# Broadcast rows read from a DRAM copy, and stationary weights stored by the host in the order of the loads

## The chip, the cores and the metric

The kernel runs on one core of a Trainium2 chip. Five engines work side by side: TensorE (PE, with its weight loads PEld), VectorE (DVE), ScalarE (ACT), GpSimd (POOL) and SyncE (SP), which in this kernel issues every DMA. The metric is the device time of one launch in microseconds, the median of several runs.

## The reference

The reference is a first attention block and two hybrid layers over 512 tokens of width 1024, in float32. What matters here is where one row of numbers is needed on all 128 partitions.

```python
# first block: FoX attention, 8 heads of 64; 16 meta tokens in front, so 528 positions
log_f = jax.nn.log_sigmoid((f_logit + b_f).astype(jnp.float32))
cum = jnp.cumsum(log_f, axis=1).transpose(0, 2, 1)
...
decay = cum[:, :, q0:q0 + Q_BLOCK, None] - cum[:, :, None, :kend]
return jnp.where(kpos[None, :] <= qpos[:, None], s + decay, NEG_INF)

# hybrid layers, branch A: mLSTM, 4 heads of 128, forward and backward
dmat = jnp.where(lower, bt[..., :, None] - bt[..., None, :] + it[..., None, :], -jnp.inf)
...
sqk = jnp.einsum('bhtd,bhsd->bhts', qt, kt) * jnp.exp(dmat - mt[..., None])
```

In FoX a term of the key alone, `-cum`, is added to the scores of each head: one row of 528 numbers, the same for all queries. In branch A the term of the key is `i[s] - B[s]`, one row of 512 numbers for each head and direction. After FoX comes MLA in the first block; after A come the branches B, C and D in each hybrid layer, an output projection and a feed-forward network (FFN) of width 2816.

## The kernel before

**Splits.** Every weight is read in float32 into a tile `raw` (three buffers of 128 x 1024, 512 KB), and `split_w` (L216 to L223) makes two parts of it: ACT writes `whi` (L220), POOL writes `wlo = raw - whi` (L222). `mm3` (L247 to L249) then does three matmuls with the parts.

**Weights as the stationary operand.** `proj_t` works on blocks of 128 output features. `w_cols` (L235) is the generator of these blocks: for a contraction over 1024 it loads a 1024 x 128 piece of the matrix with `load_w` (L232), so that each partition receives 8 runs of 128 numbers (512 bytes). For the `w_up` matrices, with a contraction over 512, a load has 4 runs of 256 numbers. `d_cols`, for branch D, gathers the two components of a head with two DMAs of 256 KB each in runs of 64 numbers. Natural projections (`proj_n`), the output projections (`proj_resid`) and `w_ffn_down` load in other ways.

**Rows.** `row_bcast` (L365) reads one SBUF row, which lies on one partition, 128 times, and writes it to all partitions:

```python
nc.sync.dma_start(dst, bass.AP(tensor=row.tensor, offset=row.offset, ap=[list(row.ap[0]), [0, P], [1, n]]))
```

FoX calls it once for each of the 8 heads, from `row` (8 partitions) to `cb`, which DVE adds to the scores (L918). Branch A calls it twice for each of 4 heads, from `arow` to `cst`; POOL adds the masks to it (L1332, tile `t`), and ACT takes exponentials of `t` and `cst` (L1349, L1352), which DVE multiplies with the scores (L1354).

**Order.** The order of TensorE is that of the program: `overlap` puts steps of the projections of later units between the steps of an attention. The other engines, and SP's DMAs, have an order that the scheduler fixes when the program is built; each runs its own list in order, so that an instruction that waits holds up what stands behind it. All DMAs are in SP's one list.

Of the kernel before, what the change touches and what calls it, by code (L numbers as in the profile page):

```python
# [18 lines left out]
P = 128  # L19
S = 512  # L20
D = 1024
KD = D // P
NT = S // P
# [7 lines left out]
# attention steps: how far the scores run ahead, and the values and the rest behind  # L31
# [6 lines left out]
# PE time given to the next work in each step after the last scores, and between the queries of branch B  # L38
# [4 lines left out]
# column offsets in the two input projections  # L43
# [4 lines left out]
# neighbourhood attention, tokens column by column: keys (in whole blocks of 128) of each tile of 128 queries  # L48
C_LO = (0, 0, 128, 256)
C_HI = (256, 384, 512, 512)  # L50
# the masks of the two inner tiles are the same
# [21 lines left out]
class Stream:  # L73
    """Projections in program order, doled out in small steps between the steps of an attention."""
# [4 lines left out]
    def push(self, gen, cost, paced=True, soon=False):  # L79
        """soon: right after the task at hand."""  # L80
        t = Task(gen, cost)
        t.paced = paced
        if soon and self.queue:
            self.queue.insert(1, t)
        else:
            self.queue.append(t)
        return t
# [26 lines left out]
    def pace(self, room, deadlines):  # L114
        """Work per unit of room, of which `room` is left, for tasks that must be done within less of it."""
# [12 lines left out]
def overlap(k, maps, look, lag, after=None, lead=4, tail=TAIL):  # L128
    """Work for after them begins with the last scores. Steps of an attention: scores run `look` maps ahead of the transposes, values and the rest `lag` behind.
    A map is (scores, transposes, values, rest, needs), needs a list of (stage, function that returns a task)."""  # L130
# [20 lines left out]
def late_steps(fns):  # L151
    """The last of the steps completes the last tile of tokens, and is not ready at once."""
    return [*fns[:-1], (0, S // 2), fns[-1], (S // 2, S)]
# [11 lines left out]
def hybrid_kernel(ctx: ExitStack, tc: tile.TileContext, i: dict, out: bass.AP):  # L165
# [40 lines left out]

    def evict_split(ps, hi, lo, scale=None):
        """hi + lo = scale * ps"""
# [7 lines left out]
    def split_w(src):  # L216
        """src [P, a, b], a * b <= 512"""
# [17 lines left out]
    def w_cols(ap, nk, c0, ncol):  # L235
        """Yields blocks of 128 output features, [P, nk, 128]."""
        width = 1024 // nk // P * P
        for a in range(0, ncol, width):
            raw = load_w(ap, 0, nk, c0 + a, min(width, ncol - a))
            for m in range(0, min(width, ncol - a), P):  # L240
                yield raw[:, :, m:m + P]

# [1 line left out]

    def mm3(ps, sh, sl, mh, ml, first, last):
        """ps += s @ m, from the parts of both"""
        T_.matmul(ps, sh, mh, start=first, stop=False)  # L247
        T_.matmul(ps, sh, ml, start=False, stop=False)  # L248
        T_.matmul(ps, sl, mh, start=False, stop=last)  # L249

    def proj_t(outs, raw, nk):
        """outs: (ps[feature, token], operand getter) for one block of features."""
# [12 lines left out]
    def proj_late(outs, ws, nk, step):  # L265
        """The same while the last tokens are still on their way: k.late lists ranges of tokens and the steps that complete them.
        The low parts of the tokens land last."""
# [12 lines left out]
    def proj_n(outs, ap, nk, c0, ncol, k0=0, more=None):  # L280
        """outs: (ps[token, ncol], operand getter); contraction over nk blocks of 128 rows of ap.
        more [P, nk, m]: the last m columns."""
# [21 lines left out]

    def rstd(ss, n, width, rows=P):
        """(ss / n + eps) ** -0.5"""
# [14 lines left out]
    # zeros, ones and powers of two are the same in both formats  # L321
# [5 lines left out]
    def softmax(src, dst):  # L327
        """dst = exp(src - max) over the row; returns its sum and the sum's reciprocal."""
# [6 lines left out]
    def softmax_banks(parts, dst):  # L335
        """The same from one or two banks (ps, first column, last); returns the sum's reciprocal."""
# [12 lines left out]
    def silu2(src, g):  # L349
        """g = 2 * silu(src) = src * (tanh(src / 2) + 1)."""  # L350
# [5 lines left out]
    def log_sigmoid(x, tmp):  # L356
        """x = min(x, 0) - log(1 + exp(-|x|))"""
# [5 lines left out]
    def row_bcast(dst, row, n):  # L363
        """One SBUF row to all partitions."""
        nc.sync.dma_start(dst, bass.AP(tensor=row.tensor, offset=row.offset, ap=[list(row.ap[0]), [0, P], [1, n]]))  # L365

# [11 lines left out]
    def to_stacks(th, tl, q, dst, n=S, off=0):  # L378
        """Split features of two heads [2*64, n]: q -> [hi; lo], k -> [hi; hi] and [lo; lo]."""
# [13 lines left out]
    class Head:  # L393
        """Attention output of one 64-wide head, [value, query], from the transposed weights of pairs of query tiles.

        v(block) -> [keys, 128] holding [v_hi | v_lo]; blocks(t) -> key blocks of query tile t."""
# [4 lines left out]
        def trans(self, t, p, col):  # L401
            """p [query, key] -> split [key, query]; col(block): first column of p."""
# [20 lines left out]
        def pv(self, t):  # L423
            """After the second tile of a pair; after the second pair the output goes to SBUF."""
# [20 lines left out]
    def pair_out(heads):  # L445
        """Outputs of two heads, [v_hi part; v_lo part] each, to one block [2*64, S]."""
# [12 lines left out]
    def y_block(yn, dst, gate=None, scale=None):  # L459
        """Natural y [P, NT, 128] to one transposed, split and gated block."""  # L460
# [10 lines left out]
    def trans_n(p):  # L471
        """p [query, S keys] -> split [key, query]"""
# [7 lines left out]
    def pv_n(pts, v):  # L480
        """ps[query, 256] = P @ [v_hi | v_lo], with the low part of P onto the first half."""
# [8 lines left out]

    def add_resid(x, t, half, ps, ss=None):
        """x += ps, and its sum of squares once x is final."""
# [10 lines left out]
    def act():  # L503
        """All positions, the meta tokens first."""
# [8 lines left out]
    def gain_row(ap, tag):  # L513
        """A gain along the features on all partitions, in halves."""
# [5 lines left out]
    def norm_tile(x, t, ss, dst, gain):  # L520
        """RMS norm of x [P, D], tile t of the tokens, into split and transposed form; returns the transposes as a second step."""
# [13 lines left out]
    def proj_resid(get, ap, k0, nk, on_tile, delay=1):  # L535
        """Natural projection to all D features that ends tile by tile; on_tile(t, halves) may return a second step, for `delay` tiles later."""
# [95 lines left out]
def first_body(k, fb, col, hl):  # L632
# [18 lines left out]
    def nat_pairs(outs, ap, nk, c0, ncol, put):  # L651
        """Tasks of a natural projection of two token tiles at a time; put(t, ps) returns a second step that follows the next pair.
        Returns the last of these steps."""
# [28 lines left out]
    # FoX forget gates: rows of -cum  # L682
    fl, ft = new(fb, [P, L], "row")[0:8], k.p_tile(L)[0:8]

    def forget(src, meta):
        """src [P, NT, 8], meta [16, 8]: natural projections"""
# [8 lines left out]
        V.tensor_scalar(fl, ft, -1.0, None, ALU.mult)  # L695

# [13 lines left out]
    def scores(t, pairs, mask):  # L710
        """128 queries against the first n positions, the mask on the last 128 of them."""
# [23 lines left out]
    qw, kw, gw = (k.w_cols(w_in, KD, c, 512) for c in (FQ, FK, FG))  # L735
# [18 lines left out]
    def fox_values():  # L754
        """With the forget gates, whose columns follow the values'."""
# [33 lines left out]
    gws = k.w_cols(w_in, KD, MG, 512)  # L789
    gates = []  # L790

    def low_rank_tile(t, ps):
        """c_q | c_kv | k_r of one tile: normed, rotated, then transposed."""
# [7 lines left out]
        # k_r lands on columns 64-95 of a block of 96  # L801
# [102 lines left out]
    def fox_head(hd):  # L904
# [5 lines left out]
        def sc(t):  # L910
            if t == 0:
                st.cb = new(pool, [P, L], "cb")
                k.row_bcast(st.cb, fl[hd:hd + 1, :], L)
# [927 lines left out]
```

## Time and profile before

| | |
|---|---|
| median of 3 runs | 2705.22 us (2703.84 to 2706.31) |
| span of the profiled execution, first to last instruction | 2704.8 us |
| mean granted TensorE clock over the span | 0.980 |
| busy: PE, DVE, ACT, POOL | 2577.5, 1333.4, 1161.4, 1286.3 us |

The time of the profiled execution itself is not among the three; its span lies 0.4 us under their median, so span and median can be used for one another here. An engine's busy time is the union of its instructions; the rest of the span it waits or has nothing to do. [...] The first block runs to about 346 us, the first hybrid layer to about 1510 us, the second to the end.

### The profile page before, as it was taken

To read this page: it belongs to the slowest core of one execution; us is meant where nothing else is said; L and a number is where in the kernel's file an instruction comes from. 1 tells how busy PE (TensorE), PEld (TensorE's weight loads), DVE (VectorE), ACT (ScalarE), POOL (GpSimd) and SP (SyncE) were. 2 spreads that over 40 slices of the span, in tenths; PEclk is the share of its full clock that TensorE was granted. 3 is DMA by queue.
4 is the path that set the end of the run, shared out by engine and by line. 5 is a ranking of instruction groups with operands and counts; after the bars stand their busy time and mean duration, and the time that the engine had idled before them with its cause. 6 is when DMAs were issued, how large, how long until landed. Compare 5 with 4: busy or idle time off the path is not lost.

```text
span 2704.8 us, 36334 instructions
## 1 busy us (share of the span) xinstructions
PE 2577.5 (95%) x12918; PEld 2137.9 (79%) x12918; DVE 1333.4 (49%) x2895; ACT 1161.4 (43%) x2533; POOL 1286.3 (48%) x1112
## 2 busy tenths in 40 slices
PE   7989987999999999999999988999999999999998
PEld 7777876787887887788888777778878878788887
DVE  3467644867645548332222347767345574322223
ACT  4457643445644445332223334356445453322223
POOL 3344243543365553545555445432655534455554
PEclk9989988999999999999999989999999999999999
DMA  5883247622346533423333367223465443333332
GB/s 142 111 136 82 59 122 80 69 87 74 90 129 164 137 92 99 137 84 100 94 94 95 108 63 87 76 83 85 126 149 140 101 106 123 95 100 94 94 94 94
DMA packets 354421, 276.81 MB, mean 102 GB/s; under 512 B 48816, under 2 KB 308144, under 8 KB 354240
## 3 DMA queue, kind: packets, MB, share of 16 engines
q1 hardware_dynamic: 354240, 274.49, 43.2%
q8 instruction: 102, 1.67, 0.3%
q14 instruction: 79, 0.65, 0.1%
HBM read 223.90 MB, written 6.29 MB: 85 GB/s over the span
## 4 chain that ended last, share of the span: by engine, by line
PE 70%; DVE 9%; DMA 8%; POOL 5%; issue 4%; ACT 3%; SPq 1%; POOLq 0%; ACTq 0%; DVEq 0%
PE A L247 15%; PE A L248 15%; PE A L249 15%; PE A L296 4%; PE A L295 4%; PE A L297 4%; PE A L313 4%; DMA raw<-in_w_in_dram 3%; PE A L440 2%; POOL wlo L222 2%; DMA raw<-in_w_out_dram 1%; DMA cst<-arow 1%; DVE ptl L211 1%; PE A L277 1%; DVE sm L330 1%
## 5 line engine op out<-in xcount | busy, mean ns | idle before, releaser
L222 POOL TENSOR_TENSOR wlo<-raw,whi 128x512 fp32r<-128x512 f32 (+2 forms) x721 | 921.8, 1281 | 937.7 <-ACT whi L220 927.7
L220 ACT CAST whi<-raw 128x512 fp32r<-128x512 f32 (+2 forms) x733 | 444.0, 608 | 805.5 <-PE A L248 435.1
L249 PE MATMUL A<-hi,wlo 128*128 128x512 f32 (+1 forms) x1848 | 729.5, 395 | 36.1 <-POOL wlo L222 30.1
L247 PE MATMUL A<-hi,whi 128*128 128x512 f32 (+1 forms) x1848 | 747.3, 404 | 7.0 <-ACT whi L220 6.3
L248 PE MATMUL A<-lo,whi 128*128 128x512 f32 (+1 forms) x1848 | 729.4, 395 | 0.4 <-DVE lo L211 0.4
L249 PEld LDWEIGHTS A<-hi,wlo 128*128 128x128 f32 x1848 | 351.8, 190 | 121.1 <-POOL wlo L222 35.6
L247 PEld LDWEIGHTS A<-hi,whi 128*128 128x128 f32 x1848 | 351.8, 190 | 73.2 <-ACT whi L220 7.6
L248 PEld LDWEIGHTS A<-lo,whi 128*128 128x128 f32 x1848 | 352.0, 190 | 64.6 <-DVE lo L211 0.6
L313 PE MATMUL A<-ident,p 128*128 128x128 f32 (+3 forms) x1125 | 180.0, 282 | 30.9 <-DVE p L524 19.7
L494 DVE TENSOR_TENSOR x<-x,A 128x512 f32<-128x512 f32 x176 | 119.9, 687 | 154.5 <-PE A L297 96.8
L313 PEld LDWEIGHTS A<-ident,p 128*128 128x128 f32 (+3 forms) x1125 | 138.6, 142 | 71.4 <-DVE p L524 19.1
L211 DVE TENSOR_TENSOR ptl<-A,pth 128x512 fp32r<-128x512 f32 (+3 forms) x256 | 148.9, 583 | 81.4 <-ACT pth L210 80.4
L331 ACT ACTIVATE p<-p,sm 128x512 f32<-128x512 f32 (+6 forms) x160 | 100.7, 629 | 173.6 <-DVE sm L330 173.3
L353 DVE SCALAR_TENSOR_TENSOR t<-t,A 128x512 f32<-128x512 f32 x44 | 30.2, 687 | 251.8 <-ACT t L352 251.8
L210 ACT CAST pth<-A 128x512 fp32r<-128x512 f32 (+3 forms) x256 | 127.3, 501 | 55.4 <-PE A L313 54.8
L309 POOL TENSOR_TENSOR rstd<-rstd,mhalf 128x1 f32<-128x1 f32 (+2 forms) x80 | 56.0, 701 | 195.6 <-DVE rstd L308 191.5
L295 PE MATMUL A<-whi,hi 128*128 128x256 f32 (+7 forms) x440 | 146.2, 332 | 0.2
L296 PE MATMUL A<-wlo,hi 128*128 128x256 f32 (+7 forms) x440 | 143.4, 326 | 2.4 <-POOL wlo L222 2.4
L297 PE MATMUL A<-whi,lo 128*128 128x256 f32 (+7 forms) x440 | 143.0, 325 | 0.0
L1064 DVE SCALAR_TENSOR_TENSOR t<-A,t 128x512 f32<-128x512 f32 x44 | 30.4, 692 | 172.0 <-PE A L249 172.0
L295 PE MATMUL A<-whi,yh 128*128 128x512 f32 x288 | 112.1, 389 | 0.0
L296 PE MATMUL A<-wlo,yh 128*128 128x512 f32 x288 | 112.1, 389 | 0.0
(365 smaller groups left out, 4572.6 us busy)
## 6 DMA issues: line engine op xcount, KB each, us to landing
raw<-in_w_in_dram SPq DMA_DIRECT2D x154, 512.0 KB, 4.0
raw<-in_w_ffn_gate_dram SPq DMA_DIRECT2D x44, 512.0 KB, 3.9
raw<-in_w_ffn_up_dram SPq DMA_DIRECT2D x44, 512.0 KB, 3.8
raw<-in_w_ffn_down_dram SPq DMA_DIRECT2D x44, 512.0 KB, 3.7
raw<-in_w_out_dram SPq DMA_DIRECT2D x24, 512.0 KB, 3.5
raw<-in_w_in_dram SPq DMA_DIRECT2D x34, 256.0 KB, 3.6
ks<-sth SPq DMA_DIRECT2D x64, 128.0 KB, 2.4
ks<-stl SPq DMA_DIRECT2D x64, 128.0 KB, 2.3
```

The costliest lines, as they stand in the source:

```text
L210: A_.copy(hi, ps)
L211: V.tensor_tensor(lo, ps, f(hi), ALU.subtract)
L220: A_.copy(hi, src)
L222: (V if k.lo and k.turn % k.lo == 0 else G).tensor_tensor(lo, src, f(hi), ALU.subtract)
L247: T_.matmul(ps, sh, mh, start=first, stop=False)
L248: T_.matmul(ps, sh, ml, start=False, stop=False)
L249: T_.matmul(ps, sl, mh, start=False, stop=last)
L295: T_.matmul(ps, sh, wh[:, j], start=(b + j == 0), stop=False)
L296: T_.matmul(ps, sh, wl[:, j], start=False, stop=False)
L297: T_.matmul(ps, sl, wh[:, j], start=False, stop=(b + j == nk - 1))
L313: T_.transpose(dst, src, ident[0:k, 0:k])
L494: V.tensor_tensor(xx, xx, ps, ALU.add)
```

## The change

Rows: the eight rows of FoX (`row`, 8 x 528) and the rows of branch A (`arow`, 36 x 512) are written once to a tile in DRAM when they are complete, and every broadcast reads its row from that copy. Weights: the host stores each matrix that `w_cols` reads as an array `t_...` in which a load is one block, and each partition's part of it is one run of 1024 numbers (4096 bytes); `d_cols` goes, and its two DMAs for a head become one. The number of bytes that are loaded is the same. Comments and docstrings are removed too, which moves line numbers.

```diff
-    def w_cols(ap, nk, c0, ncol):
-        width = 1024 // nk // P * P
-        for a in range(0, ncol, width):
-            raw = load_w(ap, 0, nk, c0 + a, min(width, ncol - a))
-            for m in range(0, min(width, ncol - a), P):
-                yield raw[:, :, m:m + P]
+    def w_cols(ap):
+        loads, _, per, nk, _ = ap.shape
+        for a in range(loads):
+            raw = raw_tile().rearrange("p (m k c) -> p m k c", m=per, k=nk)
+            nc.sync.dma_start(raw, ap[a])
+            for m in range(per):
+                yield raw[:, m]
...
-    def row_bcast(dst, row, n):
-        nc.sync.dma_start(dst, bass.AP(tensor=row.tensor, offset=row.offset, ap=[list(row.ap[0]), [0, P], [1, n]]))
+    def rows_out(rows, tag):
+        r = new(dram, list(rows.shape), tag)
+        nc.sync.dma_start(r, rows)
+        return r
...
         V.tensor_scalar(fl, ft, -1.0, None, ALU.mult)
+        fox.rows = k.rows_out(fl, "frows")
...
-    qw, kw, gw = (k.w_cols(w_in, KD, c, 512) for c in (FQ, FK, FG))
+    qw, kw, gw = (k.w_cols(i["t_" + n]) for n in ("fq", "fk", "fg"))
...
-                k.row_bcast(st.cb, fl[hd:hd + 1, :], L)
+                nc.sync.dma_start(st.cb, fox.rows[hd].partition_broadcast(P))
...
-    gw = k.w_cols(i["w_ffn_gate_2"][l], KD, 0, DFF)
-    uw = k.w_cols(i["w_ffn_up_2"][l], KD, 0, DFF)
+    gw, uw = (k.w_cols(i[n][l]) for n in ("t_gate", "t_up"))
...
         br.rows = mx, bc
+        br.arows = k.rows_out(a, "arows")
...
-                k.row_bcast(hs.ab[:, d], a[32 * d + hd:32 * d + hd + 1, :], S)
+                nc.sync.dma_start(hs.ab[:, d], br.arows[32 * d + hd].partition_broadcast(P))
...
-    def d_cols(c0):
-        for hd in range(4):
-            raw = k.raw_tile().rearrange("p (k c d) -> p k c d", k=KD, c=2)
-            for c in range(2):
-                a = c0 + 256 * c + 64 * hd
-                nc.sync.dma_start(raw[:, :, c], w.w_in[:, a:a + 64].rearrange("(k p) c -> p k c", p=P))
-            yield raw.rearrange("p k c d -> p k (c d)")
-
-    qw, kw = d_cols(DQ), d_cols(DK)
+    qw, kw = (k.w_cols(i["t_" + n][l]) for n in ("dq", "dk"))
...
+def _blocks(w, c0=0, n=None, per=1):
+    n = w.shape[-1] - c0 if n is None else n
+    *lead, rows, _ = w.shape
+    w = w[..., c0:c0 + n].reshape(*lead, rows // P, P, n // (P * per), per, P)
+    o = len(lead)
+    return np.ascontiguousarray(w.transpose(*range(o), o + 2, o + 1, o + 3, o, o + 4))
...
+    for n in "abcd":
+        out["t_up_" + n] = _blocks(g[f"w_up_{n}_2"], per=2)
+    out["t_gate"], out["t_up"] = _blocks(g["w_ffn_gate_2"]), _blocks(g["w_ffn_up_2"])
```

Apart from names and line numbers, PE, DVE and ACT keep their order. SP's and POOL's lists change at the places below.

SP's list at the start of branch A's attention in the first hybrid layer, before: two rows of each of two heads (`cst` from `arow`) stand in front of the next weight loads.

```order
L232 DMA raw_4948<-in_w_in_dram 128x8x128
L232 DMA raw_5012<-in_w_in_dram 128x8x128
L232 DMA raw_5066<-in_w_in_dram 128x8x128
L365 DMA cst_4918<-arow_4402 128x1x512 x2
L365 DMA cst_5210<-arow_4402 128x1x512 x2
L232 DMA raw_5134<-in_w_in_dram 128x8x128
L232 DMA raw_5247<-in_w_in_dram 128x8x128
L232 DMA raw_5352<-in_w_in_dram 128x8x128
L365 DMA cst_5521<-arow_4402 128x1x512 x2
```

The same place now:

```order
L240 DMA raw_4952<-in_t_aq_dram 128x1024
L240 DMA raw_5016<-in_t_ak_dram 128x1024
L240 DMA raw_5070<-in_t_ao_dram 128x1024
L367 DMA arows_4756<-arow_4404 36x512
L1334 DMA cst_4922<-arows_4756 128x512 x2
L240 DMA raw_5138<-in_t_aq_dram 128x1024
L1334 DMA cst_5214<-arows_4756 128x512 x2
L240 DMA raw_5251<-in_t_ak_dram 128x1024
L240 DMA raw_5356<-in_t_ao_dram 128x1024
L1334 DMA cst_5525<-arows_4756 128x512 x2
```

The copy (L367) is new, and the first read of it waits until it has landed; a weight load now stands ahead of the second head's rows.

POOL's list at the same place, before: `t` is the row with the mask, `wlo` the low part of a weight.

```order
L222 TENSOR_TENSOR wlo_4951<-raw_4948,whi_4950 128x512
L1332 TENSOR_TENSOR t_1038_4919<-cst_4918,masks_160 128x512
L222 TENSOR_TENSOR wlo_4967<-raw_4948,whi_4966 128x512
L1332 TENSOR_TENSOR t_1039_4920<-cst_4918,masks_160 128x512
L222 TENSOR_TENSOR wlo_5015<-raw_5012,whi_5014 128x512
```

And now:

```order
L222 TENSOR_TENSOR wlo_4955<-raw_4952,whi_4954 128x512
L222 TENSOR_TENSOR wlo_4971<-raw_4952,whi_4970 128x512
L1336 TENSOR_TENSOR t_1040_4923<-cst_4922,masks_160 128x512
L1336 TENSOR_TENSOR t_1041_4924<-cst_4922,masks_160 128x512
L222 TENSOR_TENSOR wlo_5019<-raw_5016,whi_5018 128x512
```

One `wlo` has moved ahead of the first `t`, so that it no longer stands behind the wait for a row. The second hybrid layer differs in the same way.

## Rows read from the trace of the kernel before

**Rows 1.** The page: busy time of the engines; PE and its clock in 40 slices.

```profile
PE 2577.5 (95%) x12918; PEld 2137.9 (79%) x12918; DVE 1333.4 (49%) x2895; ACT 1161.4 (43%) x2533; POOL 1286.3 (48%) x1112
...
PE   7989987999999999999999988999999999999998
...
PEclk9989988999999999999999989999999999999999
```

**Rows 2.** DMA issues: count, KB of each, median us from issue to landing.

```profile
raw<-in_w_in_dram SPq DMA_DIRECT2D x154, 512.0 KB, 4.0
...
raw<-in_w_out_dram SPq DMA_DIRECT2D x24, 512.0 KB, 3.5
...
cst<-arow SPq DMA_DIRECT2D x16, 256.0 KB, 20.3
...
cb<-row SPq DMA_DIRECT2D x8, 264.0 KB, 11.8
cb<-in_norm_dram SPq DMA_DIRECT2D x8, 256.0 KB, 3.4
...
spill<-v SPq DMA_DIRECT2D x4, 512.0 KB, 2.9
```

**Rows 3.** Chain of work that ended last, 425 to 470 us: start, us, what.

```profile
425.68 11.85 DMA cst<-arow
...
443.43 24.16 DMA raw<-in_w_in_dram
```

**Rows 4.** Timeline of POOL, 425 to 455 us: start, us, instruction, [idle before, releaser].

```profile
437.66 1.26 POOL L1332 TENSOR_TENSOR t<-cst,masks 128x512 f32<-128x512 f32 x1 [12.56 <-DMA cst<-arow]
438.88 1.26 POOL L222 TENSOR_TENSOR wlo<-raw,whi 128x512 fp32r<-128x512 f32 x1
```

**Rows 5.** Timeline of PE, branch A of the first hybrid layer.

```profile
440.20 0.79 PE L249 MATMUL A<-hi,wlo 128*128 128x512 f32 x1 [6.54 <-POOL wlo L222]
...
451.46 0.80 PE L249 MATMUL A<-hi,wlo 128*128 128x512 f32 x1 [6.07 <-POOL wlo L222]
...
468.36 0.50 PE L247 MATMUL A<-hi,whi 128*128 128x512 f32 x1 [1.80 <-ACT whi L220]
```

**Rows 6.** Timeline of PE, branch A of the second hybrid layer.

```profile
1598.77 0.80 PE L249 MATMUL A<-hi,wlo 128*128 128x512 f32 x1 [6.39 <-POOL wlo L222]
...
1608.40 0.79 PE L249 MATMUL A<-hi,wlo 128*128 128x512 f32 x1 [3.56 <-POOL wlo L222]
...
1627.82 0.80 PE L247 MATMUL A<-hi,whi 128*128 128x512 f32 x1 [4.24 <-ACT whi L220]
```

**Rows 7.** Timeline of PE in FoX.

```profile
87.52 0.52 PE L717 MATMUL A<-ks,qs 128*128 128x272 f32 x2 [1.55 <-DVE stl L214]
...
139.52 0.69 PE L313 MATMUL A<-ident,p 128*128 128x128 f32 x2 [4.95 <-DVE p L918]
...
208.72 0.47 PE L440 MATMUL A<-yl,vm 16*64 16x256 f32 x1 [2.69 <-DVE yl L211]
```

**Rows 8.** Windows, nine stretches after those idle times; first, last, sum.

```profile
88.45:91.80 3.35, 3.35 (x8) 2.22 (x8) 2.09 (x8) 2.42 (x9) 1.28 (x1) 0.50 0.96 141
...
1627.82:1631.21 3.39, 3.26 (x7) 2.15 (x8) 2.79 (x7) 1.67 (x3) 2.52 (x2) 0.50 1.14 135
sum 39.23, PE 39.09 PEld 30.52 DVE 26.45 ACT 17.50 POOL 15.43; mean PE 4.34 PEld 3.39 DVE 2.94 ACT 1.94 POOL 1.71
```

A row of windows gives start and end, length, busy time (count) of PE, PEld, DVE, ACT and POOL, the granted clock, the DMA engines' share and GB/s.

**Rows 9.** Timeline of PE, two more idle times in FoX.

```profile
168.05 0.51 PE L717 MATMUL A<-ks,qs 128*128 128x264 f32 x2 [1.28 <-DVE p L918]
...
189.83 0.51 PE L717 MATMUL A<-ks,qs 128*128 128x264 f32 x2 [1.17 <-DVE yl L211]
```

**Rows 10.** Timeline of PE, at the start of a later head of branch A.

```profile
1692.31 0.52 PE L249 MATMUL A<-hi,wlo 128*128 128x512 f32 x1 [2.24 <-POOL wlo L222]
```

**Rows 11.** Windows, a stretch of the first FFN (columns as above).

```profile
1350.00:1395.00 45.00, 45.00 (x197) 36.65 (x196) 9.60 (x14) 13.29 (x22) 24.11 (x20) 1.00 0.34 100
```

**Rows 12.** Waits: engine and line, what it waited for, us in total, times, longest.

```profile
ACT whi L220 <- DMA raw<-in_w_in_dram: 37.0, 12, 9.4
```

More of the change, by code (lines that the diff above doesn't have):

```diff
@@ L788, in first_body @@
     ckh, ckl = new(fb, [P, L], "ckh", F32R), new(fb, [P, L], "ckl", F32R)
-    gws = k.w_cols(w_in, KD, MG, 512)
+    gws = k.w_cols(i["t_mg"])
     gates = []
@@ L1114, in mixers @@
     w_in = i["w_in_2"][l]
-    glw = k.w_cols(w_in, KD, GL, 4 * D)
+    glw = k.w_cols(i["t_gl"][l])
     T_COST = 3 * KD * k.pe_cost(S)
@@ L1133, in up @@
     def up(b, y, ready=()):
-        uw = k.w_cols(i["w_up_" + "abcd"[b] + "_2"][l], 4, 0, D)
+        uw = k.w_cols(i["t_up_" + "abcd"[b]][l])
         for m in range(KD):
@@ L1296, in gate_cols @@
         A_.activation(flo, pv[:, 1], AF.Exp, scale=-1.0)
-    qw, kw, ow = (k.w_cols(w.w_in, KD, c, 512) for c in (AQ, AK, AO))
+    qw, kw, ow = (k.w_cols(i["t_" + n][l]) for n in ("aq", "ak", "ao"))
     taps = col("conv").rearrange("p (j t) -> p j t", j=8)
@@ L1571, in branch_c @@
     br.y = []
-    qw, kw, vw = (k.w_cols(w.w_in, KD, c, 512) for c in (CQ2, CK2, CV2))
+    qw, kw, vw = (k.w_cols(i["t_" + n][l]) for n in ("cq", "ck", "cv"))
     def by_col(ap):
@@ L1795, in _layout @@
            "norm1": g["norm1_g_2"], "norm2": g["norm2_g_2"]}
-    for n in ("w_in_2", "w_up_a_2", "w_up_b_2", "w_up_c_2", "w_up_d_2", "w_out_2", "w_ffn_gate_2", "w_ffn_up_2", "w_ffn_down_2"):
+    for n in ("w_in_2", "w_out_2", "w_ffn_down_2"):
         out[n] = g[n]
+    for n, c0 in (("fq", FQ), ("fk", FK), ("fg", FG), ("mg", MG)):
+        out["t_" + n] = _blocks(g["w_in"][0], c0, 512)
+    w2 = g["w_in_2"]
+    for n, c0, m in (("aq", AQ, 512), ("ak", AK, 512), ("ao", AO, 512), ("cq", CQ2, 512), ("ck", CK2, 512), ("cv", CV2, 512), ("gl", GL, 4 * D)):
+        out["t_" + n] = _blocks(w2, c0, m)
+    for n, c0 in (("dq", DQ), ("dk", DK)):
+        w = w2[:, :, c0:c0 + 512].reshape(N_LAYERS, D, 2, 4, 64).transpose(0, 1, 3, 2, 4).reshape(N_LAYERS, D, 512)
+        out["t_" + n] = _blocks(w)
+    for n in "abcd":
+        out["t_up_" + n] = _blocks(g[f"w_up_{n}_2"], per=2)
+    out["t_gate"], out["t_up"] = _blocks(g["w_ffn_gate_2"]), _blocks(g["w_ffn_up_2"])
     first = np.zeros((P, NCOL_FIRST), f32)
```

## The prediction

> **What bounds the kernel now.** I read the page first. TensorE is busy 95% of the span: 2577.5 of 2704.8 us [rows 1]. So it is the bound nearly everywhere, and a change that touches no matmul can win at most the 127 us in which it stands still, and the time that it loses at the low clock level. The slices tell where these lie: PE is below 9 tenths, and its granted clock below full, at the start, in FoX (slices 2 and 3, about 135 to 270 us), in branch A of the first hybrid layer (slices 5 and 6) and in branch A of the second (slices 23 and 24). In between both rows are nines.
>
> The table of DMA issues says what is special in FoX and branch A. A row broadcast of 256 KB takes 20.3 us in the median from issue to landing, one of 264 KB in FoX 11.8 us, while weight loads of 512 KB land in 3.5 to 4.0 us [rows 2]. The chain of work that ended last shows both sides of it at the start of branch A: the first broadcast, issued at 425.68 us, is waited for 11.85 us, and a weight load issued at 443.43, behind four of them, takes 24.16 us instead of 4.0 [rows 3]. So the transfers of one SBUF row are slow, and the queue behind them is late too.
>
> The timeline of POOL links this to TensorE: POOL stands 12.56 us at the first `t` (L1332) until the row has landed, and the next `wlo` stands behind it [rows 4]. TensorE, whose matmul needs that `wlo`, is idle 6.54 us, then 6.07 us at the second broadcast, then 1.80 us for the late weight load [rows 5]. The second hybrid layer repeats it with 6.39, 3.56 and 4.24 us [rows 6]. In FoX three idle times follow a broadcast: 1.55 us (at the split of a projection whose weights were queued behind two rows), 4.95 us and 2.69 us (at what DVE makes of scores and `cb`) [rows 7].
>
> [...]
>
> **The change part by part.** *The rows' idle time.* It removes the slow reads. The nine idle times sum to 6.54 + 6.07 + 1.80 = 14.41, 6.39 + 3.56 + 4.24 = 14.19 and 1.55 + 4.95 + 2.69 = 9.19, in all 37.8 us [rows 5 to 7].
>
> *The clock after them.* Work at half the clock takes twice its time, so half of 39.09 us, 19.5 us, comes back if TensorE no longer stops there [rows 8]. Gross gain: 57.3 us.
>
> *What is added.* Three copies of rows to DRAM, and a wait for each in SP's list before the first read; behind that wait stand the other row reads and the next weight loads. The trace has no such small copy. From above, a store of 512 KB to DRAM lands in 2.9 us [rows 2]; from below it is nothing. I take the upper end, since the size is small against what makes up that time in no row I have. A broadcast out of DRAM is in the trace: a 256 KB gain row, read for all partitions by the same call, lands in 3.4 us [rows 2]. So the first row of a group is there 2.9 + 3.4 = 6.3 us after `arow` is ready instead of 11.85, and the others right behind it instead of some 10 us later each.
>
> Does that close the 6.54 us? TensorE ran dry at 440.20 - 6.54 = 433.7 us. In the new order one `wlo` more is done before POOL stands at `t`; it feeds 12 matmuls of 0.23 us (45.00 us for 197, [rows 11]), 2.7 us, to 436.4. The row lands at 425.7 + 6.3 = 432.0, two `t` and a `wlo` take 3 x 1.26 us [rows 4], which gives 435.8. So this wait goes, narrowly, and the second and third, for later rows and the queue, with room.
>
> *What stays.* At later heads of branch A, where the row had landed long before, TensorE still stops up to 2.24 us, since POOL does two `t` and another subtraction ahead of the `wlo` [rows 10]. The same can now show at the two first heads in each layer: 0 to 2.24 us, four times, 0 to 9 us. I take 1 us each, 4 us, since the arithmetic above comes out near zero for the first head. Such a stop can again cost a stretch at the half clock: I take 2 us in all, and up to 7 us. Sum of what stays: 6 us, at most 16.
>
> *Two more idle times in FoX*, 1.28 and 1.17 us, follow DVE and ACT work that was late behind broadcasts, but also behind other work [rows 9]. I take half, 1.2 us, with 0 to 2.45 as bounds.
>
> *The weight layout.* A load in 4 KB runs already exists: `w_out`, 512 KB in 3.5 us, against 4.0 us for `w_in` in runs of 512 bytes [rows 2]. So each changed load may land 0.5 us sooner. That is worth nothing where a load has cover: three buffers of `raw` let SP issue a load two loads ahead of its use, and in the FFN TensorE is busy 45.00 of 45.00 us [rows 11]. If the cover is gone, it is worth 0.5 us per wait: ACT waited 12 times for such a load, 37.0 us in all [rows 12], mostly behind rows and counted above. Bounds 0 to 6 us; I take 0, as ACT's other waits have slack before PE. [...]
>
> *Sum.* 57.3 - 6 + 1.2 + 0 = 52.5 us. The profiled span is 0.4 us under the median, so I take it off the median: 2705.2 - 52.5 = 2652.7, say **2653 us**. Best case: 57.3 + 2.45 + 6 = 65.8 us, 2639. Worst case of this mechanism: 57.3 - 16 and half of FoX's part lost (its 9.19 and half of its 12.8 us at the low clock make 15.6; half is 7.8), 33.5 us, 2672.
>
> **The rivals.** *A: another engine takes the place.* DVE, ACT and POOL are busy 43 to 49% of the span [rows 1], in FoX and branch A in chains of small instructions, and their lists are in order. If each row wait turned into waits on these chains, only the waits over 4 us would go (6.54, 6.07, 6.39, 4.24, 4.95: 28.2 us), half of that given back later, and half of the clock's part: 14 + 10 = 24 us, 2681. For it: the residual stops [rows 10]. Against it: these engines stood still themselves during the waits, POOL for 12.56 us at a time [rows 4], so they have the time.
>
> *B: the reads stay slow*, because 128 reads of one row meet in one place of DRAM as they met in one partition. Then only the layout is left: 0 to 6 us, 2702, within noise or just out of it. The gain row's 3.4 us speaks against it [rows 2]: same call, same size, also one row read 128 times. [...]
>
> *C: slower, by the weight loads.* The FFNs read 88 changed loads (22 blocks, gate and up, two layers) while TensorE has no slack at all [rows 11]. If a load in 4 KB runs landed so late that its cover was gone, each would stop TensorE. The gain of 52.5 us is used up when a load is 0.6 us late beyond its cover, at 88 x 0.6 = 53 us; at 1 us late the time is 2705 + 35 = 2740. Against it: `w_out` in such runs lands sooner, not later [rows 2].
>
> **How the numbers follow.** My forecast (33 to 66 us faster): 0.74. A (10 to 33 us): 0.14. More than 66 us, if other small stops in FoX go too: 0.06. B: 0.03. C: 0.03. The range reaches half of A: 2632 to 2678. 0.2% of the time is 5.4 us, about what a measurement can tell from no change. Faster takes the forecast, A and the larger gain, 0.94, and a little of B: 0.95; the same 0.02, slower 0.03.
>
> **What the profile after would show.** Row broadcasts landing in 3 to 5 us, copies in under 3 us; no wait of POOL for `cst` above 7 us; the six idle times of branch A gone or under 2.3 us; granted clock near 1.00 in the slices of branch A; changed weight loads at about 3.5 us, with the FFN windows unchanged at 197 matmuls in 45 us. Wrong if the broadcasts land in 10 us or more (B), if PE's idle time in branch A stands under other names, DVE or POOL (A), or if the FFN windows hold fewer matmuls (C).

## The result, and the profile after

| | before | after |
|---|---|---|
| median of 4 runs each, us | 2704.5 (2701.6 to 2706.3) | 2637.6 (2636.2 to 2640.0) |
| ratio, 95% interval | | 0.9753 (0.9740 to 0.9767) |
| span of the profiled execution, us | 2704.8 | 2635.8 |

The kernel is 66.9 us faster, where 52.5 us were forecast; 2637.6 lies in the range of 2632 to 2678, but past the best case of 65.8 us (2639). The first place to look is the page of the changed kernel, beside [rows 1].

```profile
PE 2554.8 (97%) x12918; PEld 2127.0 (81%) x12918; DVE 1334.6 (51%) x2895; ACT 1162.8 (44%) x2533; POOL 1291.5 (49%) x1112
...
PE   7999989999999999999999999999999999999998
...
PEclk9999999999999999999999999999999999999999
```

The dents of FoX and of both branches A are gone; slice 5 (counted from 0), before branch A begins, keeps its 8. The page also splits the 69.0 us of the two spans. The span less TensorE's busy time was 2704.8 - 2577.5 = 127.3 us and is 2635.8 - 2554.8 = 81.0: 46.3 us less standing still. The busy time itself fell by 22.7 us with the same 12918 matmuls. Most of that is the clock: windows over every stretch with a granted clock of 0.50 (a share of full speed), their sums before and after:

```profile
sum 107.66, PE 86.94 PEld 73.61 DVE 59.01 ACT 45.58 POOL 38.27; mean PE 3.95 PEld 3.35 DVE 2.68 ACT 2.07 POOL 1.74
...
sum 57.02, PE 52.76 PEld 44.69 DVE 32.88 ACT 19.47 POOL 19.18; mean PE 3.52 PEld 2.98 DVE 2.19 ACT 1.30 POOL 1.28
```

TensorE did 86.9 us of work at that level before and does 52.8 us now. Half of the difference, 17.1 us, is my estimate of what the clock gave back: at the first head of branch A in the changed kernel, matmuls of one size started 0.43 us apart at a granted clock of 0.50 (411.4 to 414.4 us) and 0.23 us apart at 1.00 (414.8 to 421.7 us), about twice as far. The cause of the other 5.6 us is not shown. Fewer stops may be part of it (72 of over 0.1 us instead of 100), since the matmul at 468.36 in [rows 5], behind a stop of 1.80 us, lasted 0.50 us, and the one at 419.46 below, with no stop before it, 0.39.

The DMA issues answer to [rows 2] (count, KB of each, median us from issue to landing):

```profile
raw<-in_t_gate_dram SPq DMA_DIRECT2D x44, 512.0 KB, 3.4
...
cst<-arows SPq DMA_DIRECT2D x16, 256.0 KB, 4.6
...
cb<-frows SPq DMA_DIRECT2D x8, 264.0 KB, 3.9
```

Rows land in 4.6 and 3.9 us instead of 20.3 and 11.8. POOL's timeline at the first head of branch A answers to [rows 4] (start, us, instruction, idle before and what ended it):

```profile
406.13 1.83 POOL L222 TENSOR_TENSOR wlo<-raw,whi 128x512 fp32r<-128x512 f32 x1 [1.06 <-ACT whi L220]
411.80 1.27 POOL L1336 TENSOR_TENSOR t<-cst,masks 128x512 f32<-128x512 f32 x1 [3.84 <-DMA cst<-arows]
413.36 1.28 POOL L1336 TENSOR_TENSOR t<-cst,masks 128x512 f32<-128x512 f32 x1 [0.29 <-DMA cst<-arows]
414.60 1.29 POOL L222 TENSOR_TENSOR wlo<-raw,whi 128x512 fp32r<-128x512 f32 x1
```

POOL waits 3.84 us where it waited 12.56. TensorE there and at the last head:

```profile
409.18 0.22 PE L314 MATMUL A<-ident,p 36*128 36x36 f32 x1 [1.00 <-DVE p L1288]
...
419.46 0.39 PE L250 MATMUL A<-hi,wlo 128*128 128x512 f32 x1
...
490.21 0.80 PE L250 MATMUL A<-hi,wlo 128*128 128x512 f32 x1 [2.25 <-POOL wlo L222]
```

The matmul at 419.46 is the one that stood still 6.07 us in [rows 5]; nothing precedes it now. Its `wlo` was ready at 414.60 + 1.29 = 415.89, so the slack is 3.6 us. The stop of 2.25 us at the last head (behind POOL's fourth pair of `t`, at 484.18 us) is of the kind in [rows 10], which is the same place in the second layer.

Since TensorE's order is the same in both kernels, a stretch can be cut at the same two instructions. Windows of FoX and the two branches A, first of the kernel before (start and end, length, busy time and count of PE, PEld, DVE, ACT and POOL, granted clock, DMA share, GB/s):

```profile
80.00:245.96 165.96, 148.67 (x839) 123.48 (x838) 105.52 (x301) 90.20 (x247) 71.37 (x76) 0.92 0.71 122
424.98:599.93 174.95, 149.46 (x766) 122.75 (x765) 116.17 (x309) 70.54 (x154) 80.42 (x73) 0.94 0.60 73
1580.02:1760.01 179.99, 156.31 (x797) 129.34 (x796) 119.58 (x311) 71.04 (x155) 84.45 (x75) 0.92 0.58 71
```

and of the changed kernel:

```profile
81.12:227.96 146.84, 139.54 (x840) 118.47 (x838) 106.15 (x299) 90.02 (x245) 69.64 (x76) 0.97 0.45 128
404.94:557.92 152.98, 145.93 (x766) 122.28 (x765) 116.70 (x309) 70.49 (x154) 81.95 (x73) 0.96 0.26 84
1535.70:1691.97 156.27, 148.20 (x798) 124.75 (x796) 120.26 (x311) 71.09 (x155) 85.79 (x75) 0.97 0.26 83
```

FoX is 19.1 us shorter, the two branches A 22.0 and 23.7; that leaves 69.0 - 64.8 = 4.2 us for the rest of the program. VectorE, ScalarE and POOL are as busy as before in the shorter stretches, and the DMA engines' share in branch A falls from 0.60 to 0.26. The FFN is what it was in [rows 11], again 197 matmuls in 45 us:

```profile
1309.00:1354.00 45.00, 45.00 (x197) 36.65 (x196) 9.59 (x14) 13.29 (x22) 24.15 (x20) 1.00 0.29 94
```

### The profile page after: what moved, and what is told of

It reads as the page before. It is cut to its first block, busy times and chain, and to the rows that moved or that the text cites. A ratio compares the mean times of both kernels' runs of the same rounds, so it can differ in the third digit from the quotient of the medians.

```text
span 2635.8 us, 36300 instructions
## 1 busy us (share of the span) xinstructions
PE 2554.8 (97%) x12918; PEld 2127.0 (81%) x12918; DVE 1334.6 (51%) x2895; ACT 1162.8 (44%) x2533; POOL 1291.5 (49%) x1112
## 4 chain that ended last, share of the span: by engine, by line
PE 75%; DVE 10%; POOL 4%; issue 4%; DMA 3%; ACT 2%; SPq 0%; POOLq 0%; DVEq 0%; ACTq 0%
PE A L248 17%; PE A L249 16%; PE A L250 16%; PE A L296 5%; PE A L297 5%; PE A L298 5%; PE A L314 4%; PE A L443 3%; POOL wlo L222 2%; DMA raw<-in_w_out_dram 1%; DVE ptl L211 1%; DMA cb<-in_c_rpb_z_dram 1%; PE A L488 1%; DVE sm L331 1%; PE A L278 1%
## 5 line engine op out<-in xcount | busy, mean ns | idle before, releaser
L497 DVE TENSOR_TENSOR x<-x,A 128x512 f32<-128x512 f32 x176 | 120.0, 688 | 154.0 <-PE A L298 96.8
L314 PEld LDWEIGHTS A<-ident,p 128*128 128x128 f32 (+3 forms) x1125 | 135.7, 139 | 67.2 <-DVE p L527 19.1
L332 ACT ACTIVATE p<-p,sm 128x512 f32<-128x512 f32 (+6 forms) x160 | 100.7, 629 | 155.2 <-DVE sm L331 154.0
```

Source lines behind the costliest of these rows:

```text
L314: T_.transpose(dst, src, ident[0:k, 0:k])
L497: V.tensor_tensor(xx, xx, ps, ALU.add)
```

## The experiments

Each stretch is measured as above, between the same TensorE instructions, from one profile of each kernel; the rest is the span less the three. The ratio is to the kernel before.

| kernel | ratio (95%) | FoX | branch A, 1st | branch A, 2nd | rest |
|---|---|---|---|---|---|
| before | | 166.0 | 175.0 | 180.0 | 2183.9 |
| changed | 0.9753 (0.9740 to 0.9767) | 146.8 | 153.0 | 156.3 | 2179.7 |
| changed, again | 0.9751 (0.9733 to 0.9769) | 143.2 | 153.1 | 156.5 | 2180.8 |
| rows alone | 0.9744 (0.9731 to 0.9756) | 143.0 | 150.8 | 155.0 | 2183.3 |
| layout alone | 0.9989 (0.9980 to 0.9997) | 164.0 | 174.1 | 178.1 | 2177.2 |
| rows of branch A alone | 0.9828 (0.9815 to 0.9842) | 166.9 | 151.0 | 156.8 | 2183.4 |
| slow rows on ScalarE's queue | 1.0084 (1.0065 to 1.0102) | 182.9 | 177.7 | 181.1 | 2183.6 |
| changed, second copy | 0.9769 (0.9757 to 0.9782) | 149.5 | 154.0 | 157.2 | 2181.0 |
| changed, runs of 512 B | 0.9776 (0.9762 to 0.9790) | 147.1 | 153.5 | 157.2 | 2189.3 |

**Rows alone.** The kernel before with the new row code and the old weights:

```
+        fox.rows = k.rows_out(fl, "frows")
+        br.arows = k.rows_out(a, "arows")
-                k.row_bcast(st.cb, fl[hd:hd + 1, :], L)
+                nc.sync.dma_start(st.cb, fox.rows[hd].partition_broadcast(P))
-                k.row_bcast(hs.ab[:, d], a[32 * d + hd:32 * d + hd + 1, :], S)
+                nc.sync.dma_start(hs.ab[:, d], br.arows[32 * d + hd].partition_broadcast(P))
```

> The row copies and the reads out of DRAM alone; the weights in the old layout (runs of 512 bytes). Theory R (rows alone): nearly the whole gain of 66.9 us, 2638 to 2642 us, weight loads landing in 4.0 us, the stretches of FoX, branch A and branch A of the second layer gaining about 18, 22 and 23 us as in the changed kernel. Theory R+ (rows in these three stretches, layout at the phase changes near 380, 1520 and 2010 us): 63.5 us, about 2641 us, and those three changes gain nothing. Rival L (the 14 us beyond the forecast are the layout's): 2652 us.

It took 2634.8 us, below all three expectations. The rows are the whole gain within what the runs can tell, and rival L falls. These runs change the reads and, with them, the order of POOL's list; no run takes the two apart. From the rows the order alone would not do: the `wlo` of the next weight, for which TensorE stood still until 451.46 us in [rows 5], stands behind both `t`, and so behind both rows, in either order. The DMA issues of rows alone:

```profile
raw<-in_w_in_dram SPq DMA_DIRECT2D x154, 512.0 KB, 3.7
...
cst<-arows SPq DMA_DIRECT2D x16, 256.0 KB, 4.9
```

The same loads in runs of 512 bytes that took 4.0 us in [rows 2] land in 3.7: part of the 0.5 us that I had put down to the layout seems to have been the rows' doing. Far from any row, in the FFN, the gate's loads still take 3.8 us here and 3.4 in the changed kernel.

**Layout alone.** The changed kernel with `row_bcast` from the SBUF row put back in both places.

> The new weight layout alone; rows still read from the one SBUF partition. Theory R: within 0.1% of the kernel before, 2701 to 2705 us, row broadcasts still 20 and 12 us, changed weight loads 3.5 us where nothing is queued ahead. R+: 3 to 6 us faster, 2698 to 2701 us, all of it at the phase changes. Rival L: 14 us faster, 2690 us. Rival C of the prediction (loads in 4 KB runs late): slower than before.

2700.8 us, 3.0 us less by its ratio of 0.9989. The gain is small, and its interval ends at 0.9997. Rows still take 20.6 and 11.8 us, most changed loads 3.5. Rivals L and C fall: away from the rows no load in 4 KB runs is late (those of the FFN's gate land in 3.4 us). Whether the 3 us are real and lie at the phase changes (R+) stays open.

**Rows of branch A alone.** As rows alone, without the two edits in FoX.

> The kernel before with the copy and the DRAM reads for the rows of branch A alone; FoX's rows stay slow, weights in the old layout. If the stretches are independent, as the cumulative gain of the two profiles says (18 us in FoX, 22.0 and 23.5 us in the two branches A): 45 us faster, 2656 to 2663 us. If the small stops of branch A that went too were the new weight layout's and not the rows': 35 us faster, about 2670 us, as the forecast's own terms for branch A.

2657.8 us, 47 us less, the upper expectation. FoX stays at 166.9 us while both branches A are as short as in the changed kernel, with the old weights. So the stretches are independent, and most of the small stops of branch A went with its rows, not with the layout.

**Slow rows on another queue.**

```
-        nc.sync.dma_start(dst, bass.AP(tensor=row.tensor, ...
+        nc.scalar.dma_start(dst, bass.AP(tensor=row.tensor, ...
```

> The kernel before, with the slow row reads issued by ScalarE on its own DMA queue instead of SP's. Theory Q (the weight loads were late only because they stood behind rows in one queue): weight loads land in about 4 us again, rows still take 11 us for the first and longer for the others, TensorE's third stop of each branch A (1.80 and 4.24 us) goes, the first stays at about 6 us; 2680 to 2700 us. Rival E (slow packets hold up the transfer engines, whichever queue they came from): weight loads issued next to rows still take well over 8 us, 2700 to 2710 us. Rival S (ScalarE itself stands at these issues): slower than before.

2727.6 us, slower. The DMA issues of the stretch 440 to 500 us, where weight loads on SP's queue (q1) run beside rows on ScalarE's (q10):

```profile
q10 hardware_dynamic: 863, 1.57, 79.9%
...
raw<-in_w_in_dram SPq DMA_DIRECT2D x6, 512.0 KB, 17.3
cst<-arow ACTq DMA_DIRECT2D x6, 256.0 KB, 18.9
```

The rows keep the engines busy 79.9% of the time with 1.57 MB, and weight loads that share no queue with them take 17.3 us. Theory Q falls, rival E stands: the slow reads hold up the engines, not only the list they stand in. Loads also stand behind one another in SP's queue here; the next run has one load by itself. Rival S came true as well. ScalarE's timeline and TensorE's behind it:

```profile
459.04 0.62 ACT L220 CAST whi<-raw 128x512 fp32r<-128x512 f32 x1 [16.37 <-issue]
```

```profile
459.71 0.80 PE L247 MATMUL A<-hi,whi 128*128 128x512 f32 x1 [10.48 <-ACT whi L220]
```

ScalarE stands 16.37 us at its own row issues (two of them, from 442.07 us, take 16.87 us), and TensorE 10.48 us for the `whi` behind them.

**Transfers by themselves.** A kernel that computes nothing of the model: it only moves rows and adds them up. `src` reads one row out of each of `n` partitions that lie `step` apart, 128 / n times each; `add` lets VectorE add the tile up, so that each of these broadcasts waits for the one before.

```
+        for n, step in ((1, 1), (4, 1), (4, 4), (16, 8), (128, 1)):
+            for _ in range(4):
+                nc.sync.dma_start(t, rows[:, :] if n == P else src(rows[0:1], n, step, P // n))
+                add(t)
+        for _ in range(4):
+            nc.sync.dma_start(t, cp[5].partition_broadcast(P))
```

> Transfers by themselves, nothing of the model computed: 256 KB broadcasts of one row out of one SBUF partition, out of four neighbouring partitions (0 to 3), out of four that lie four apart (0, 4, 8, 12), out of 16 that lie eight apart, from each partition to itself, out of one DRAM row; then four broadcasts and a weight load behind them, in one queue and in two. [...] Rival N (the single partition limits): four neighbours take a quarter, 4 us. Rival B of the prediction (a DRAM row is slow as well): 11 us for the DRAM row. The weight load behind four slow rows: about 40 us in the same queue; in the other queue 4 us if only the queue was in the way, over 10 us if the engines were.

Its chain of work, one transfer of each kind, in that order (start, us from issue to landing, what), then the DRAM row and a weight load:

```profile
3.79 11.15 DMA t<-rows
...
64.36 12.03 DMA t<-rows
...
102.61 4.42 DMA t<-rows
...
123.80 2.98 DMA t<-rows
...
138.93 2.29 DMA t<-rows
...
151.36 2.99 DMA t<-cp
...
167.13 3.16 DMA wsolo<-in_t_fq_dram
```

One source partition takes 11.15 us, four neighbouring ones no less (12.03), four that lie four apart 4.42, sixteen that lie eight apart 2.98, and the DRAM row 2.99; it is one execution, and the four transfers of a kind agree within 0.4 us. So it is not the single partition that limits, as rival N had it: four partitions took 12.03 us as neighbours and 4.42 us when they lay four apart. Something that neighbours share seems to limit; no run shows what. Rival B of the prediction falls by the 2.99 us of the DRAM row.

VectorE's timeline shows four rows of single partitions issued together:

```profile
196.65 0.69 DVE L186 TENSOR_TENSOR acc<-acc,sbsame 128x512 f32<-128x512 f32 x1 [10.56 <-DMA sbsame<-rows]
206.29 0.69 DVE L186 TENSOR_TENSOR acc<-acc,sbsame 128x512 f32<-128x512 f32 x1 [8.94 <-DMA sbsame<-rows]
```

They land 9.6 us apart. The weight load behind them was done at 226.1 us, some 41 us after the first issue; behind four DRAM rows it landed 5.45 us after its own issue. What a second queue does is in the same trace. A load on ScalarE's queue (q10) is issued at 228.67 us, with four slow rows on SP's (q1), the first issued at 227.33. Its issue; the queues' packets (count, MB, share of the engines) from there until VectorE has the first row, at 239.17; and from there until it has the second, at 249.06:

```profile
228.67 0.37 ACTq L215 DMA_DIRECT2D wsbother<-in_t_fq_dram  x1
...
q1 hardware_dynamic: 161, 0.30, 92.2%
...
q1 hardware_dynamic: 145, 0.26, 85.3%
q10 hardware_dynamic: 144, 0.52, 13.0%
```

Not one packet of the load moves in the first 10.5 us, and all 144 move in the next 9.9, though its queue is its own. Beside four DRAM rows all 144 moved within 6.9 us of the issue. So rival E is shown here by itself.

**A second copy.** The changed kernel with the rows of branch A copied twice before they are read.

```
-        br.arows = k.rows_out(a, "arows")
+        br.arows = k.rows_out(k.rows_out(a, "arows"), "arows2")
```

> The changed kernel with a second copy, DRAM to DRAM, chained between the first copy of the rows of branch A and the reads; the rows land later by one copy, estimated at 2 us from the 1.75 us of the first. If the first head has slack only by a hair, as the prediction's 435.8 against 436.4 us says: TensorE stops 1 to 2 us more at the first head of each layer, with some us at the half clock behind it, 2 to 8 us slower than the changed kernel, 2640 to 2646 us. If the slack is larger (over 2 us): no change, 2637 to 2639 us.

2641.5 us, inside the range expected for a slack "by a hair"; but the slack had measured 3.6 us, and the interval overlaps the changed kernel's. The branches A are 1.0 and 0.9 us longer, no stop returned at the first head of the first layer, and FoX, which has the same code, is 2.7 us longer too. It isn't a clean test of the slack: the scheduler put one more weight load, and one more `wlo` on POOL, ahead of the rows.

**Short runs in one block.** The host stores each block such that each partition's part is eight runs of 512 bytes.

```
-    return np.ascontiguousarray(w.transpose(*range(o), o + 2, o + 1, o + 3, o, o + 4))
+    return np.ascontiguousarray(w.transpose(*range(o), o + 2, o, o + 3, o + 1, o + 4))
```

> The changed kernel with the blocks of the weights still one piece of DRAM each, but their inner order such that each partition's part is eight runs of 512 bytes (the loads of the two-block up projections stay as changed). If the length of a run sets 3.5 against 4.0 us: loads land in 4.0 us. If it was the distance between the runs (24 KB rows of the old matrix): 3.5 us. The time by theory R: 2637 to 2640 us in either case.

```profile
raw<-in_t_gl_dram SPq DMA_DIRECT2D x64, 512.0 KB, 4.1
raw<-in_t_gate_dram SPq DMA_DIRECT2D x44, 512.0 KB, 4.0
```

Loads take 4.0 to 4.1 us instead of 3.4 to 3.5, so the length of the runs, or their number, counts here, by 0.6 us a load. The time, 2644.8 us, lies above the 2637 to 2640 us that were expected in either case, with an interval that overlaps the changed kernel's; what is longer lies outside the three stretches (the rest, 2189.3 us), and the cause was not followed up.

**The stop at the last head.** (The second expectation calls it the second head's; it is the fourth pair of `t` that stands before it.) One of POOL's two `t` goes to VectorE, or both.

```
-                G.tensor_tensor(hs.am[d], hs.ab[:, d]...
+                (G if d else V).tensor_tensor(hs.am[d], hs.ab[:, d]...
```

> The changed kernel with the first of the two mask additions of each head of branch A on VectorE instead of GpSimd, so that GpSimd's list has one addition of 1.27 us less ahead of the low part of a weight. If GpSimd's list sets the stops at the later heads (2.25 us at 488 us, 2.24 us at 1622 us): each shrinks by about 1.3 us and half-clock work behind it goes in part, 2 to 6 us faster, 2632 to 2636 us. Rival (VectorE's chain of small instructions is late instead): the stops that follow VectorE (1.75 us at the last head) grow, no change or slower, 2637 to 2642 us.

> The changed kernel with both mask additions of each head of branch A on VectorE. One of them there shrank the stop at the second head from 2.25 to 1.24 us and gave 2629.2 against 2637.8 us. If GpSimd's list alone sets that stop: it is gone (under 0.4 us), 2 to 4 us less again, 2625 to 2628 us. If VectorE's chain takes over: the scans and transposed weights of the later maps are late, new stops behind VectorE of over 0.5 us in branch A, 2630 us or more.

One moved: 2629.2 us (0.9725, 0.9705 to 0.9745). TensorE's stop:

```profile
487.08 0.50 PE L250 MATMUL A<-hi,wlo 128*128 128x512 f32 x1 [1.24 <-POOL wlo L222]
```

Both moved: 2633.1 us (0.9735, 0.9722 to 0.9749):

```profile
485.45 0.50 PE L250 MATMUL A<-hi,wlo 128*128 128x512 f32 x1 [0.31 <-POOL wlo L222]
487.01 0.81 PE L314 MATMUL A<-ident,p 128*128 128x128 f32 x4 [1.06 <-DVE p L1366]
491.01 0.33 PE L489 MATMUL A<-v,ptl 128*128 128x128 f32 x1 [1.00 <-DVE ptl L211]
```

The mechanism is shown: POOL's list sets that stop, 2.25, then 1.24, then 0.31 us, and with both gone VectorE is late instead at 487.01 us. (The stop at 491.01 is no sign of it: the second profile of the changed kernel has it too, 1.00 us at 493.77.) Whether it gains time was asked twice more, without the layout and once again as it was:

> Rows out of DRAM and the first mask addition of each head on VectorE, with the weights in the old layout: the best version without the layout. If the layout is worth nothing on top of the rows: ratio to the kernel before within 0.002 of the 0.9725 that rows, layout and the moved addition gave together, 2625 to 2636 us, loads of the old layout landing in 3.7 us. If the layout is worth the 3 us that it gave alone: 0.9735 or more.

> The changed kernel with the first mask addition on VectorE once more, since the same move without the weight layout gave nothing (0.9752 against 0.9744). If its 0.9725 was the move's and the layout's together: 0.9715 to 0.9735 again. If it was the scatter of the half-clock stretches behind small stops: 0.974 to 0.9765, as the changed kernel itself.

0.9752 (0.9739 to 0.9765) and 0.9740 (0.9726 to 0.9754). So the 0.9725 did not come back, and no version that beats the changed kernel is shown. The three measurements with a `t` moved and the new layout (0.9725, 0.9740, 0.9735) all lie below the changed kernel's 0.9753 and 0.9751, with intervals that overlap; a gain of 3 to 5 us is not excluded.

**The scatter itself.** The changed kernel, run and profiled again.

> The changed kernel as it is, beside the others of this call: 2635 to 2640 us; FoX's stop of 1.96 us at 153 us and of 1.46 us at 194 us again, since the order of instructions is the same; what TensorE loses at the half clock behind such a stop of 1 to 2 us may differ from the first profile (there 6.8 us of half clock behind the first of them).

2637.8 us, the same median. The two profiles differ in FoX, 146.8 against 143.2 us, with one program. TensorE's stop in FoX and a window of 10 us over it, first profile, then second:

```profile
154.87 0.51 PE L721 MATMUL A<-ks,qs 128*128 128x264 f32 x2 [1.96 <-DVE p L922]
```

```profile
152.50:162.50 10.00, 8.04 (x30) 6.14 (x29) 7.37 (x20) 5.27 (x15) 2.26 (x2) 0.66 0.29 82
```

```profile
154.01 0.51 PE L721 MATMUL A<-ks,qs 128*128 128x264 f32 x2 [1.95 <-DVE p L922]
```

```profile
152.10:162.10 10.00, 8.09 (x56) 7.22 (x57) 8.85 (x25) 6.59 (x18) 2.88 (x3) 1.00 0.43 114
```

The stop is the same. Behind it the granted clock was 0.66 over the window in the first, with 30 matmuls, and 1.00 in the second, with 56; a second stop, of 1.46 us at 194 us, is in the first profile alone.

## Why the prediction was right, and where it was off

**The mechanism was right.** Row reads were slow since their source lay in one partition (by themselves 11.15 us, 12.03 from four neighbours, 2.99 from a DRAM row), and dear since they delayed POOL (12.56 us at the first `t` [rows 4]), VectorE (8.88 us, below) and the weight loads (24.16 us [rows 3]) alike. Rows alone give the whole gain, as far as the runs resolve it, branch A alone its own share. Eight of the nine stops of [rows 5 to 7] are gone, and the ninth, FoX's 2.69 us, is 0.56 us. One correction: I told the lateness of the weight loads as a queue's. The run with the rows on ScalarE's queue and the transfers by themselves show that a load in another queue is late too: 17.3 us beside rows on ScalarE's, and no packet moved for 10.5 us where the load had its queue to itself. A second one: I put FoX's 4.95 us down to `cb`. VectorE stood there for a transfer of 128 KB of its own, issued at 126.69 us behind a row issued at 126.13:

```profile
138.56 0.68 DVE L451 TENSOR_TENSOR t<-t,t 64x512 f32<-64x512 f32 x1 [8.88 <-DMA t<-t]
```

A third, without weight for the sum: of the slices that I read as dents, slice 3 shows 9 in both rows, and slice 5 (338 to 406 us) ends before branch A begins.

**The first head.** The sum held: `wlo` was forecast 10.1 us after `arow` is ready and came 10.2 us after (415.89 against 405.65), the row 6.0 us after instead of 6.3. The copy takes under 1.8 us (the first read is issued at 407.4), not 2.9, and the read 4.3, not 3.4. "Narrowly" was wrong: TensorE asks for that `wlo` 13.8 us after `arow`, not 10.7. It had 15 instructions of matmul work in between, not 12, and TensorE itself arrived 2.3 us later, behind the stop of 1.00 us for VectorE's scan and some 1.4 us of work at the low clock (matmuls 0.43 us apart instead of 0.23). So the first head has slack in part because something else made TensorE late.

**The term that failed is the small stops, which I put at nothing.** In the stretches, idle time is the window's length less PE's busy time. It fell by 18.4 and 15.6 us in the branches A, 34.0 in all, against 14.41 + 14.19 - 4 = 24.6 forecast. Instruction by instruction, the six stops that I listed gave their 28.6 us. "What stays" came out near its 4 us, though not where I put it: 3.0 us are new, about 1.0 us at VectorE's scan in each layer and 1.0 us more at the last head of the first. But other stops, which I had not listed, shrank by 8.5 us. Four of the kernel before, of which the first is gone, the second is 0.29 us, the third became the 2.25 us above, and the last is in the second profile of the changed kernel but not in the first:

```profile
502.61 0.50 PE L249 MATMUL A<-hi,wlo 128*128 128x512 f32 x1 [1.49 <-POOL wlo L222]
...
528.82 0.33 PE L486 MATMUL A<-v,ptl 128*128 128x128 f32 x1 [1.49 <-DVE ptl L211]
...
532.28 0.51 PE L249 MATMUL A<-hi,wlo 128*128 128x512 f32 x1 [1.23 <-POOL wlo L222]
...
537.23 0.33 PE L486 MATMUL A<-v,ptl 128*128 128x128 f32 x1 [1.00 <-DVE ptl L211]
```

I took such stops for the heads' own, because the engine named was POOL or VectorE. With branch A's rows alone, weights as before, they shrank by 6.6 us, so most of this hung on the rows. The amount moves by itself: in the second profile of the changed kernel it is 5.8 us.

**The clock.** I let 19.5 - 2 = 17.5 us come back; by the sums of the windows at 0.50 above it is 17.1 us. The size was right, the account was not: my nine windows hold 39 of the 87 us that TensorE worked at that level, and 53 us of such work are still there. Busy time fell by 5.6 us more than the clock explains, a term that I did not have, and the second profile shows that each part moves by some us between executions.

**FoX's idle time** fell by 17.3 - 7.3 = 10.0 us, against 9.19 + 1.2 = 10.4. Of the two stops of [rows 9], of which I had taken half, 1.17 us went, and 1.28 us became the 1.96 us at 153 us. That the sum fits is in part luck: other stops shrank by 4.5 us and new ones of 3.1 us came.

**The rest, and the layout.** For the rest of the program I had forecast nothing; it is 4.2 us shorter. The layout alone gives 3.0 us, inside its bounds of 0 to 6 and below what I said a measurement can tell. On top of the rows it isn't resolved: 0.9753 and 0.9751 with it, 0.9744 without.

**The rivals.** A falls: no engine took the rows' place; the largest stops behind VectorE in the three stretches are 1.96 and 1.75 us. B and C fall by the runs above. My forecast's own class, 33 to 66 us, was missed by 1 us: 66.9 us is in the class that I gave 0.06, and its reason, small stops in FoX, was the wrong place for most of them. The miss of 14.4 us adds up over the page's two parts: standing still 46.3 instead of 35.0 (9.4 us of it in the branches A), busy time 22.7 instead of 17.5, less 2.1 us between spans and medians.

## What to carry to other kernels

When a DMA reads one SBUF partition for all others, price it by what it does to every transfer beside it, not by its own wait: here a weight load behind four such reads took 24.16 us, and loads beside them on another queue 17.3, against 3.8 to 4.0 us in the medians of those kernels. A copy to DRAM and a broadcast from there cost 6.0 us for the first row, and POOL waited 0.29 us more for the second. When a slow transfer goes, expect small stops behind engines of the same stretch to shrink with it, as here by 5.8 and 8.5 us in the branches A of two profiles, and a few new ones to come (3.0 us there in the first). Don't read gains of a few us from two profiles: time the kernel again, since one program's FoX differed by 3.7 us between two.

## What the runs showed of the hardware that was not expected

- Slow reads held up loads in another queue: 17.3 us for a weight load with the rows on ScalarE's queue, 3.8 us in the median of that kernel; and a single load on a queue of its own, with no packet moved for 10.5 us.
- Runs of 512 bytes landed later from one packed block (4.0 to 4.1 us) than from the old matrix with its long rows (3.7 to 3.8 us, rows alone). The cause stays open.
- Behind a stop of nearly the same length (1.96 and 1.95 us) the granted clock over 10 us was 0.66 in one execution and 1.00 in the other.
- The second of two scans at the first head ran longer when a `wlo` of POOL lay beside it. VectorE's timeline, before and after:

```profile
425.69 2.44 DVE L1285 TENSOR_TENSOR_SCAN p<-arow 4x512 f32<-4x512 f32 x2
```

```profile
405.65 3.38 DVE L1288 TENSOR_TENSOR_SCAN p<-arow 4x512 f32<-4x512 f32 x2
```

  That `wlo` took 1.83 us instead of 1.29. Before, POOL stood still at that time [rows 4]; but an earlier pair of scans, which had a `wlo` beside it in the kernel before too, was as long there:

```profile
419.05 3.53 DVE L1282 TENSOR_TENSOR_SCAN p<-p 4x512 f32<-4x512 f32 x2 [0.61 <-POOL p L1278]
```

  It is so in every trace of the model's kernels, 13 in all: the 46 scans of this size that start while a `wlo` runs take 2.15 to 2.31 us, the 58 others 1.21 to 1.22. No run moved one of them on purpose. So the stop of 1.0 us at the scan seems to be a price of the faster rows: POOL now has its `wlo` there.
